# An encoder block's recurrent half: two-tensor work taken from GpSimd to VectorE, its steps dealt anew over eight chunks

## The chip, the core and the metric

The kernel runs on one core of a Trainium2 chip. TensorE (PE) multiplies matrices; VectorE (DVE), ScalarE (ACT) and GpSimd (POOL) work elementwise; SyncE (SP) issues most of the transfers. Each of them executes its own list of instructions in order and waits on semaphores. The metric is the device time of one execution in microseconds. Three runs of the kernel before gave 1787.31, 1787.67 and 1789.67 us: the median is 1787.67 us.

## What is computed

One encoder block on 512 tokens of width 2048. An RMS-normalised input is projected by one wide matrix into the inputs of two branches: a bidirectional recurrent branch (RWKV-7, 16 heads of 64 channels) and a grouped-query attention branch. Both are gated, projected and merged, and a last projection, a residual and a norm follow. The change lies in the recurrent branch. Cut to what matters:

```python
def _wkv_step(S, inp):                       # S: 64 x 64 state of a head and a direction
    w, kk, b, k, v, r = inp
    sa = jnp.einsum('dbhvk,dbhk->dbhv', S, -kk)
    S = S * w[..., None, :] + sa[..., None] * b[..., None, :] + v[..., :, None] * k[..., None, :]
    o = jnp.einsum('dbhvk,dbhk->dbhv', S, r)
    return S, o
...
    kkh = kkh * lax.rsqrt(jnp.maximum(jnp.sum(kkh * kkh, axis=-1, keepdims=True), 1e-24))
    k_eff = _heads(k[None] * (1.0 + (a - 1.0) * k_a.astype(f32)))
    seq_in = (decay, kkh, kkh * ah, k_eff, vh, rh)   # each for both directions
    _, outs = lax.scan(_wkv_step, S0, seq_in)
    wkv = outs[0] + jnp.flip(outs[1], axis=1)
    mu = jnp.mean(wkv, axis=-1, keepdims=True)
    var = jnp.mean(jnp.square(wkv - mu), axis=-1, keepdims=True)
    gn = (wkv - mu) * lax.rsqrt(var + GN_EPS)
...
    return x + jnp.einsum('btd,de->bte', merged, w_out)
```

## The kernel before

**The dense stream.** The wide projection is a stream of products of 128x128 by 128x512 (line 291, tile `acc`). Each weight tile `raw` of four 128x128 blocks is split into a high part `wh` (ACT, line 264) and a rest `wl` (DVE, line 265); twelve products use one such tile, and three tiles of each kind are kept. A *planner* (class `Weave`) writes the PE's order out by hand: each task of the recurrent branch is a generator that yields a cost in planner nanoseconds, a wait, and a flag it needs, and wherever no task is due the planner puts a dense product. The order of DVE, ACT, POOL and SP is made by a scheduler from the order in which the code issues instructions.

**The recurrent branch** goes over eight tiles of 128 channels (two heads), two directions, and eight chunks of 64 tokens:

- `stage_a(i)` makes the decay sums, keys and rates of tile i. `pss` (line 507) sums squares for the key norm, `prb` (516) spreads it. Its elementwise work is cut into seven steps. For tile 0 they run by themselves; for tile i+1 step n runs within chunk n of tile i. `exclusive` (528), `rate` (541), `keys` (544) and the sum of keys (592) are operations with two tensors on POOL; the three exponentials (549 to 551) are on ACT, the products into `BK` (562) on DVE.
- `tile_task(i)` starts with products into `AL` (618 on DVE; 621 on DVE for one direction, on POOL for the other), then `lr` (633) with masks on DVE (636 to 640), a split of `ks` whose rest `cl_` is made on POOL, and a triangular inversion of 60 small DVE operations in series (676, 677) that ends in `XX` (691, 694), which `pq` (709) reads. Then comes the loop over chunks: `pa` (747) reads the state `SV`; ACT copies its result into `a0s` (749, 750), which `pu` (756) reads; ACT copies that into `SV` (757, 758), which `px` (763) reads; DVE makes the next state from it in four operations (769). POOL puts the values of a chunk into `SV` (742) and clears its state part at the start (736, 737).
- `stage_e(i)` norms the output of tile i while tile i+1 is under way: a chain of DVE, ACT and POOL operations that ends in `ow` (802), which the PE transposes (`pg`, 809).

**What sets places around the change.** `OPT` has planner waits: `gn` is the time between the norm's issue and `pg`, `subwait` that between the inversion's transposes and `pq`. `behind(mv, mn, mo)` tells the scheduler to issue a step after three given instructions: the last write of values, the last state operation and the last output copy.

Of the kernel before, what the change touches and what calls it, by code (L numbers as in the profile page):

```python
# [8 lines left out]
F32 = mybir.dt.float32  # L9
# [10 lines left out]
C = 64  # L20
# [190 lines left out]
        return True  # L211


OPT = dict(manual=True, tls=True, sub="dve", subwait=46000, fwait=6000, gn=15000, u1=0, u2=0, c1=700, c2=700, c3=1400, fly=3, scale='pool', prb=4, low=1300, warm=24, rwt='tile', every=2, auto=1, man=1)


def context(nc):
# [7 lines left out]
def emit_all(nc, tc, A, out, dbg):  # L225
# [263 lines left out]
    def stage_a(i):  # L489
# [11 lines left out]
        sq = temp("sq")  # L501
        ac.activation(sq, k, AF.Square, scale=pc(P_KK + i))
        ac.activation(kk, k, AF.Copy, scale=pc(P_KK + i))
        yield 0, 1500, None
        pss = g_tile("pss")
        for tt in range(4):
            pe.matmul(pss[:, 2 * tt:2 * tt + 2], lhsT=sq[:, tt * 128:(tt + 1) * 128], rhs=hs2, start=True, stop=True)
# [12 lines left out]
        def scan(d):  # L520
            h["cs", d] = temp("cs0") if d == 0 else rw.tile([128, T], F32, name="cs1")
            ve.tensor_tensor_scan(h["cs", d], rst, la[:, d], 0.0, ALU.mult, ALU.add)
            if d == 1:
                cs = h["cs", 1]
                ve.tensor_tensor(out=ch(cs), in0=ch(cs)[:, :, C - 1:C].to_broadcast([128, NC, C]), in1=ch(cs), op=ALU.subtract)

        def exclusive(d):
            po.tensor_tensor(out=la[:, d], in0=h["cs", d], in1=la[:, d], op=ALU.subtract if d == 0 else ALU.add)  # L528

            h["in", d], h["ex", d] = (h["cs", d], la[:, d]) if d == 0 else (la[:, d], h["cs", d])  # L530

        def effective(d):
            if d == 0:
                h["ks"] = rw.tile([128, T], F32, name="ks", bufs=2)
                h["BK"] = rw.tile([128, 2, NC, 128], F32, name="BK", tag="bko")
                h["PC"] = rw.tile([128, 2, NC], F32, name="PC", bufs=2)
            h["ke", d] = h["ks"] if d == 0 else temp("ke1")
            ve.tensor_scalar(out=h["ke", d], in0=la[:, 2 + d], scalar1=pc(P_KA + i), scalar2=oka[:, i:i + 1], op0=ALU.mult, op1=ALU.add)

        def rate(d):  # L540
            po.tensor_tensor(out=la[:, 2 + d], in0=la[:, 2 + d], in1=kk, op=ALU.mult)

        def keys(d):
            po.tensor_tensor(out=h["ke", d], in0=h["ke", d], in1=k, op=ALU.mult)

        def exps(d):
            ci, ce = h["in", d], h["ex", d]
            h["e2", d] = rw.tile([128, T], F32, name=f"e2{d}")
            ac.activation(h["e2", d], ci, AF.Exp, scale=-HS)
            ac.activation(ci, ci, AF.Exp, scale=HS)  # L550
            ac.activation(ce, ce, AF.Exp, scale=-HS)

        def ends(d):
            e2 = ch(h["e2", d])
# [3 lines left out]
        def decayed(d, s0):  # L558
            src = la[:, 2 + d] if s0 == 0 else h["ke", d]
            for h0 in (0, 64):  # L560
                sl = s0 if h0 == 0 else 1 - s0
                ve.tensor_tensor(out=h["BK"][h0:h0 + 64, d, :, sl * C:(sl + 1) * C], in0=ch(src)[h0:h0 + 64], in1=ch(h["in", d])[h0:h0 + 64], op=ALU.mult)

        def step(n):
            if n == 0:
                ve.tensor_scalar(out=la, in0=la, scalar1=0.5, scalar2=0.5, op0=ALU.mult, op1=ALU.add)
                scan(0)
            elif n == 1:
                exclusive(0)
                scan(1)  # L570
                effective(0)
            elif n == 2:
                exps(0)
                exclusive(1)
                keys(0)
                effective(1)
                rate(0)
            elif n == 3:
                exps(1)
                keys(1)  # L580
                rate(1)
                decayed(0, 0)
                ends(0)
            elif n == 4:
                ends(1)
                decayed(0, 1)
            elif n == 5:
                decayed(1, 0)
            else:
                decayed(1, 1)  # L590
                ks = h["ks"]
                po.tensor_tensor(out=ks, in0=ks, in1=h["ke", 1], op=ALU.add)
                ve.scalar_tensor_tensor(out=ks, in0=r, scalar=pc(P_RK + i), in1=ks, op0=ALU.mult, op1=ALU.mult)
                fact[i] = (kk, ks, [(h["ex", d], h["e2", d]) for d in range(2)], h["BK"], h["PC"])
                W.flag(f"A{i}", 4000)
# [11 lines left out]
    def tile_task(i):  # L607
# [7 lines left out]
        for d in range(2):  # L615
            e1, e2 = dirs[d]
            for h0, eo, sl in ((0, 0, 0), (64, 1, 1)):
                ve.scalar_tensor_tensor(out=AL[h0:h0 + 64, d, :, eo, sl * C:(sl + 1) * C], in0=ch(kk)[h0:h0 + 64], scalar=-1.0,
                                        in1=ch(e1)[h0:h0 + 64], op0=ALU.mult, op1=ALU.mult)
            for h0, eo, sl in ((0, 0, 1), (64, 1, 0)):  # L620
                (po if d else ve).tensor_tensor(out=AL[h0:h0 + 64, d, :, eo, sl * C:(sl + 1) * C], in0=ch(r)[h0:h0 + 64], in1=ch(e2)[h0:h0 + 64], op=ALU.mult)
        yield 0, OPT['fwait'], None

        LB = rw.tile([128, 2, NC, C], F32, name="LB", tag="lb")
# [27 lines left out]
        VT = rw.tile([128, 4, 128], F32, name="VT", bufs=1)  # L652
        ac.copy(VT, pv.rearrange("p (j c) -> p j c", j=4))
        ch_, cl_ = temp("ch_", F32R), temp("cl_", F32R)
        split(ch_, cl_, ks, po)

        FT = rw.tile([128, 2, NC, 32], F32, name="FT", tag="ft")
        for q in range(4):
# [68 lines left out]
        yield 450, 0, f"N{i + 1}" if i < NT - 1 else None  # L727

        O = rw.tile([128, 2, 2 * NC, C], F32, name="O", tag="lb")
        SV = None  # L730
        for n in range(NC):
            cc = (n, NC - 1 - n)
            both = slice(n, 2 * NC - n, 2 * NC - 1 - 2 * n)
            if SV is None:
                SV = rw.tile([128, 2, 2, 2, C], F32, name="SV", bufs=2)
                po.memset(SV[0:64, :, 0, 0, :], 0.0)
                po.memset(SV[64:128, :, 1, 0, :], 0.0)
            for d in range(2):
                rv = (cc[d] % 2) * 64
                for eo, v0 in ((0, 64), (1, 0)):  # L740
                    src = VT[rv:rv + 64, cc[d] // 2, eo * C:(eo + 1) * C]
                    mv = po.tensor_scalar(out=SV[v0:v0 + 64, d, eo], in0=src.unsqueeze(1).to_broadcast([64, 2, C]),  # L742
                                     scalar1=1.0, scalar2=0.0, op0=ALU.mult, op1=ALU.add)
            pa = c_tile("pa").rearrange("p (d e x) -> p d e x", d=2, e=4)
            for d in range(2):
                for eo in range(2):
# [15 lines left out]
                for eo in range(2):  # L762
                    pe.matmul(px2[:, d, eo, :], lhsT=L2[:, d, cc[d], eo, :], rhs=SV[:, d, eo, 1, :], start=True, stop=True)  # L763
            if n < NC - 1:
                SN = rw.tile([128, 2, 2, 2, C], F32, name="SV", bufs=2)
                for d in range(2):
                    for eo in range(2):
                        h = slice(64 * eo, 64 * eo + 64)
                        mn = ve.scalar_tensor_tensor(out=SN[h, d, eo, 0, :], in0=SV[h, d, eo, 0, :], scalar=PC[h, d, cc[d]:cc[d] + 1], in1=px2[h, d, eo, :], op0=ALU.mult, op1=ALU.add)  # L769
                SV = SN  # L770
# [393 lines left out]
```

## Time and profile before

| | |
|---|---|
| median of three runs | 1787.67 us |
| profiled execution | 1786.3 us |
| its span, first to last instruction | 1784.5 us |
| PE busy | 1708.5 us (96%) |
| DVE busy | 1215.2 us (68%) |
| ACT busy | 849.6 us (48%) |
| POOL busy | 494.7 us (28%) |
| mean granted clock of the PE | 0.982 |

The recurrent stage with its chunk loops lies between about 60 and 1190 us; attention with the rest of the dense stream follows, and the last projection ends the program. A tile of the recurrent stage takes about 132 us. Products overlap in the PE, so that a busy PE can still run at half its clock; the granted clock has to be read beside the busy time.

### The profile page before, as it was taken

To read this page: it belongs to the slowest core of one execution; us is meant where nothing else is said; L and a number is where in the kernel's file an instruction comes from. 1 tells how busy PE (TensorE), PEld (TensorE's weight loads), DVE (VectorE), ACT (ScalarE), POOL (GpSimd) and SP (SyncE) were. 2 spreads that over 40 slices of the span, in tenths; PEclk is the share of its full clock that TensorE was granted. 3 is DMA by queue.
4 is the path that set the end of the run, shared out by engine and by line. 5 is a ranking of instruction groups with operands and counts; after the bars stand their busy time and mean duration, and the time that the engine had idled before them with its cause. 6 is when DMAs were issued, how large, how long until landed. Compare 5 with 4: busy or idle time off the path is not lost.

```text
span 1784.5 us, 26149 instructions
## 1 busy us (share of the span) xinstructions
PE 1708.5 (96%) x8972; PEld 1433.3 (80%) x8972; DVE 1215.2 (68%) x2356; ACT 849.6 (48%) x1955; POOL 494.7 (28%) x604
## 2 busy tenths in 40 slices
PE   7999998999999989999999999999999999999997
PEld 6788877887877877887877877888787888788886
DVE  6567768769779778768668768634878876543342
ACT  5555445355355355455445354444567655332241
POOL 2021051051051061061051051013546542431110
PEclk8999999999999999999999999999999999999999
DMA  6563323313323313324323323325424322434452
GB/s 217 160 204 118 100 63 95 112 55 111 98 64 112 102 54 113 95 54 119 97 57 106 101 60 95 110 71 164 128 77 148 107 91 82 149 113 147 131 181 106
DMA packets 96852, 194.89 MB, mean 109 GB/s; under 512 B 11088, under 2 KB 11344, under 8 KB 95312
## 3 DMA queue, kind: packets, MB, share of 16 engines
q1 hardware_dynamic: 77616, 152.18, 29.4%
q10 hardware_dynamic: 15264, 28.46, 4.5%
q0 software_dynamic: 3840, 12.59, 2.4%
q8 instruction: 72, 1.18, 0.3%
q14 instruction: 60, 0.49, 0.1%
HBM read 162.77 MB, written 30.41 MB: 108 GB/s over the span
## 4 chain that ended last, share of the span: by engine, by line
PE 52%; DVE 6%; ACT 2%; issue 2%; DMA 1%; POOL 1%; POOLq 0%; DVEq 0%; ACTq 0%
PE acc L291 33%; PE of L1095 2%; PE of L1096 2%; PE of L1094 2%; PE px L763 2%; PE po L986 2%; PE pT L971 1%; PE pa L747 1%; DVE wl L265 1%; PE pu L756 1%; PE sc L954 1%; PE sc L955 1%; PE acc L1094 1%; PE acc L1096 1%; PE acc L1095 1%
## 5 line engine op out<-in xcount | busy, mean ns | idle before, releaser
L291 PE MATMUL acc<-hh,wl 128*128 128x512 f32 (+1 forms) x1388 | 555.0, 400 | 2.8 <-DVE wl L265 2.6
L291 PE MATMUL acc<-hl,wh 128*128 128x512 f32 (+1 forms) x1388 | 554.4, 399 | 2.4 <-DVE hl L386 2.1
L291 PE MATMUL acc<-hh,wh 128*128 128x512 f32 (+1 forms) x1388 | 555.7, 400 | 0.0
L265 DVE TENSOR_TENSOR wl<-raw,wh 128x512 fp32r<-128x512 f32 x441 | 340.3, 774 | 282.0 <-ACT wh L264 261.9
L264 ACT CAST wh<-raw 128x512 fp32r<-128x512 f32 x472 | 291.8, 620 | 458.1 <-PE acc L291 314.8
L291 PEld LDWEIGHTS acc<-hh,wl 128*128 128x128 f32 x1388 | 265.5, 191 | 54.7 <-DVE wl L265 5.2
L291 PEld LDWEIGHTS acc<-hl,wh 128*128 128x128 f32 x1388 | 265.4, 191 | 53.5 <-DVE hl L386 3.5
L291 PEld LDWEIGHTS acc<-hh,wh 128*128 128x128 f32 x1388 | 265.5, 191 | 49.9 <-ACT wh L264 0.3
L742 POOL TENSOR_SCALAR SV<-VT 64x128 f32<-64x128 f32 x256 | 123.8, 484 | 584.7 <-DVE SV L769 261.4
L769 DVE SCALAR_TENSOR_TENSOR SV<-SV,PC,px 64x64 f32<-64x64 f32 x224 | 62.7, 280 | 68.2 <-PE px L763 51.1
L676 DVE TENSOR_TENSOR tm<-B 128x30 f32<-128x30 f32 (+14 forms) x240 | 82.1, 342 | 4.8
L291 PE MATMUL acc<-oq,wh 128*128 128x512 f32 x256 | 83.1, 396 | 2.0 <-ACT oq L1018 1.3
L677 DVE TENSOR_TENSOR B<-B,tm 128x30 f32<-128x30 f32 (+14 forms) x240 | 79.0, 329 | 5.4
L747 PEld LDWEIGHTS pa<-SV,AL 128*128 128x128 f32 x512 | 67.7, 191 | 16.5 <-POOL la L528 8.5
L747 PE MATMUL pa<-SV,AL 128*128 128x64 f32 x512 | 67.4, 271 | 9.4 <-DVE SV L769 9.4
L1095 PE MATMUL of<-wl,mh 128*128 128x512 f32 x192 | 74.9, 390 | 0.2
L1096 PE MATMUL of<-wh,ml 128*128 128x512 f32 x192 | 74.7, 389 | 0.0
L763 PEld LDWEIGHTS px<-SV,L 128*128 128x128 f32 x512 | 68.6, 195 | 7.1 <-ACT SV L757 1.6
L1094 PE MATMUL of<-wh,mh 128*128 128x512 f32 x192 | 66.1, 389 | 0.0
L763 PE MATMUL px<-SV,L 128*128 128x64 f32 x512 | 66.0, 273 | 0.1
L771 ACT COPY O<-px 64x128 f32<-64x128 f32 x64 | 16.7, 261 | 100.4 <-DVE SV L769 89.9
L756 PEld LDWEIGHTS pu<-a0s,XP 128*128 128x128 f32 x256 | 37.1, 194 | 25.1 <-ACT a0s L750 20.4
(687 smaller groups left out, 2844.9 us busy)
## 6 DMA issues: line engine op xcount, KB each, us to landing
raw<-in_w_in_dram SPq DMA_DIRECT2D x344, 256.0 KB, 3.2
raw<-in_wo_dram SPq DMA_DIRECT2D x64, 256.0 KB, 2.8
fsp<-tg ACTq DMA_DIRECT2D x60, 256.0 KB, 2.4
tsp<-la ACTq DMA_DIRECT2D x32, 256.0 KB, 3.6
la<-tsp SPq DMA_DIRECT2D x8, 1024.0 KB, 5.6
raw<-in_wbr_dram SPq DMA_DIRECT2D x32, 256.0 KB, 3.1
tgm<-fsp POOLq DMA_DIRECT2D x32, 256.0 KB, 3.6
raw<-in_wba_dram SPq DMA_DIRECT2D x32, 256.0 KB, 2.9
```

Of the source, the lines that this page charges most:

```text
L264: ac.copy(dst_hi, src)
L265: (eng or ve).tensor_tensor(out=dst_lo, in0=src, in1=f(dst_hi), op=ALU.subtract)
L291: pe.matmul(acc[:, tok], lhsT=w[1 if u == 2 else 0][:, j, :], rhs=(xl if u == 1 else xh)[:, kt, tok], start=(kt == 0 and u == 0 and tok.st ...
L676: se.tensor_tensor(out=tv, in0=B[:, 0:s, s:s + 1].to_broadcast([128, s, n]), in1=B[:, s:s + 1, s + 1:32].to_broadcast([128, s, n]), op=ALU ...
L677: se.tensor_tensor(out=B[:, 0:s, s + 1:32], in0=B[:, 0:s, s + 1:32], in1=tv, op=ALU.add)
L742: mv = po.tensor_scalar(out=SV[v0:v0 + 64, d, eo], in0=src.unsqueeze(1).to_broadcast([64, 2, C]), scalar1=1.0, scalar2=0.0, op0=ALU.mult, ...
L747: pe.matmul(pa[:, d, eo, :], lhsT=AL[:, d, cc[d], eo, :], rhs=SV[:, d, eo, 0, :], start=True, stop=True)
L763: pe.matmul(px2[:, d, eo, :], lhsT=L2[:, d, cc[d], eo, :], rhs=SV[:, d, eo, 1, :], start=True, stop=True)
L769: mn = ve.scalar_tensor_tensor(out=SN[h, d, eo, 0, :], in0=SV[h, d, eo, 0, :], scalar=PC[h, d, cc[d]:cc[d] + 1], in1=px2[h, d, eo, :], op0 ...
L1094: pe.matmul(acc, lhsT=mh[:, dt, tok(tt)], rhs=w[0], start=(dt == 0), stop=False)
L1095: pe.matmul(acc, lhsT=mh[:, dt, tok(tt)], rhs=w[1], start=False, stop=False)
L1096: pe.matmul(acc, lhsT=ml[:, dt, tok(tt)], rhs=w[0], start=False, stop=(dt == NKT - 1))
```

## The change

All operations with two tensors that POOL did in `stage_a` and `tile_task` are issued on DVE: `exclusive`, `rate`, `keys`, the sum of keys, the second direction of the `AL` products and the rest `cl_` of the split. For each tile these are ten operations (two, two, two, one, two, one); POOL keeps the values of the state, the 8-column copies `PC`, small powers and its transfers. The seven steps are dealt anew: two exponentials of a direction stay together in `exp_in`, the third of both directions goes to step 4 (`exp_ex`); `exclusive(1)` stays in step 2, `rate` moves one step later. The values of chunk n+1 are written (`state`) ahead of the state operations of chunk n, and the steps are issued behind these writes. Three planner waits grow: `gn` from 15000 to 22000, `subwait` from 46000 to 47000, and for tile 0 the wait ahead of `pss` from 1500 to 6000.

```diff
-OPT = dict(..., subwait=46000, fwait=6000, gn=15000, ...)
+OPT = dict(..., subwait=47000, fwait=6000, gn=22000, ...)
...
-        yield 0, 1500, None
+        yield 0, 1500 if i else 6000, None
...
         def exclusive(d):
-            po.tensor_tensor(out=la[:, d], in0=h["cs", d], in1=la[:, d], op=ALU.subtract if d == 0 else ALU.add)
+            ve.tensor_tensor(out=la[:, d], in0=h["cs", d], in1=la[:, d], op=ALU.subtract if d == 0 else ALU.add)
...
-            po.tensor_tensor(out=la[:, 2 + d], in0=la[:, 2 + d], in1=kk, op=ALU.mult)
+            ve.tensor_tensor(out=la[:, 2 + d], in0=la[:, 2 + d], in1=kk, op=ALU.mult)
...
-            po.tensor_tensor(out=h["ke", d], in0=h["ke", d], in1=k, op=ALU.mult)
+            ve.tensor_tensor(out=h["ke", d], in0=h["ke", d], in1=k, op=ALU.mult)
...
-        def exps(d):
-            ci, ce = h["in", d], h["ex", d]
+        def exp_in(d):
+            ci = h["in", d]
             h["e2", d] = rw.tile([128, T], F32, name=f"e2{d}")
             ac.activation(h["e2", d], ci, AF.Exp, scale=-HS)
             ac.activation(ci, ci, AF.Exp, scale=HS)
-            ac.activation(ce, ce, AF.Exp, scale=-HS)
+
+        def exp_ex(d):
+            ac.activation(h["ex", d], h["ex", d], AF.Exp, scale=-HS)
...
+            elif n == 2:
+                exp_in(0)
+                exclusive(1)
                 effective(0)
-            elif n == 2:
-                exps(0)
-                exclusive(1)
                 keys(0)
                 effective(1)
+            elif n == 3:
+                exp_in(1)
+                ends(0)
                 rate(0)
-            elif n == 3:
-                exps(1)
                 keys(1)
+                decayed(0, 0)
+            elif n == 4:
+                exp_ex(0)
+                exp_ex(1)
+                ends(1)
                 rate(1)
-                decayed(0, 0)
-                ends(0)
-            elif n == 4:
-                ends(1)
                 decayed(0, 1)
...
-                po.tensor_tensor(out=ks, in0=ks, in1=h["ke", 1], op=ALU.add)
+                ve.tensor_tensor(out=ks, in0=ks, in1=h["ke", 1], op=ALU.add)
...
-                (po if d else ve).tensor_tensor(out=AL[h0:h0 + 64, d, ...], in0=ch(r)[h0:h0 + 64], in1=ch(e2)[h0:h0 + 64], op=ALU.mult)
+                ve.tensor_tensor(out=AL[h0:h0 + 64, d, ...], in0=ch(r)[h0:h0 + 64], in1=ch(e2)[h0:h0 + 64], op=ALU.mult)
...
-        split(ch_, cl_, ks, po)
+        split(ch_, cl_, ks)
...
+        def state(n):
+            new = rw.tile([128, 2, 2, 2, C], F32, name="SV", bufs=2)
+            for d, c in ((0, n), (1, NC - 1 - n)):
+                ...
+                    mv = po.tensor_scalar(out=new[v0:v0 + 64, d, eo], in0=src.unsqueeze(1).to_broadcast([64, 2, C]),
+                                          scalar1=1.0, scalar2=0.0, op0=ALU.mult, op1=ALU.add)
+            return new, mv
+
+        SV, _ = state(0)
...
-                SN = rw.tile([128, 2, 2, 2, C], F32, name="SV", bufs=2)
+                SN, mv = state(n + 1)
```

**How it moves the work.** DVE, chunk loop of the third tile (the one whose trace stands below around 501 us), from the third state update on. `SV` is the next state, `la` holds sums and rates, `cs` the running sums, `ks` and `ke` the keys, `BK` products for the next tile. Before:

```order
L769 SCALAR_TENSOR_TENSOR SV<-SV,PC,px_4656 64x64 x4
L538 TENSOR_SCALAR ke_4674<-la,par,der 128x512
L265 TENSOR_TENSOR wl<-raw,wh 128x512
L769 SCALAR_TENSOR_TENSOR SV<-SV,PC,px_4717 64x64 x4
L562 TENSOR_TENSOR BK<-la,cs_4547 64x8x64 x2
L265 TENSOR_TENSOR wl<-raw,wh 128x512 x2
L769 SCALAR_TENSOR_TENSOR SV<-SV,PC,px_4782 64x64 x4
L562 TENSOR_TENSOR BK<-ks,cs_4547 64x8x64 x2
L265 TENSOR_TENSOR wl<-raw,wh 128x512
```

The changed kernel at the same place:

```order
L776 SCALAR_TENSOR_TENSOR SV<-SV,PC,px_4679 64x64 x4
L528 TENSOR_TENSOR la<-cs_4637,la 128x512
L538 TENSOR_SCALAR ks<-la,par,der 128x512
L538 TENSOR_SCALAR ke_4704<-la,par,der 128x512
L544 TENSOR_TENSOR ks<-ks,k 128x512
L265 TENSOR_TENSOR wl<-raw,wh 128x512
L776 SCALAR_TENSOR_TENSOR SV<-SV,PC,px_4749 64x64 x4
L541 TENSOR_TENSOR la<-la,kk 128x512
L544 TENSOR_TENSOR ke_4704<-ke_4704,k 128x512
L564 TENSOR_TENSOR BK<-la,cs_4582 64x8x64 x2
L265 TENSOR_TENSOR wl<-raw,wh 128x512
```

Between the third and the fourth state update stand five instructions where two stood; `exclusive` (528), `keys` (544) and `rate` (541) are those that came from POOL.

ACT in the same loop, after the fourth chunk's output copies; `e` takes an exponential, `a0s` is what `pu` waits for. Before:

```order
L771 COPY O<-px_4717 64x2x64
L772 COPY O<-px_4717 64x2x64
L549 ACTIVATE e_4729<-la 128x512
L551 ACTIVATE cs_4609<-cs_4609 128x512
L476 DMA fsp<-tg 128x512
L749 COPY a0s<-pa 64x128
L750 COPY a0s<-pa 64x128
```

The changed kernel:

```order
L778 COPY O<-px_4749 64x2x64
L779 COPY O<-px_4749 64x2x64
L549 ACTIVATE e_4765<-la 128x512
L550 ACTIVATE la<-la 128x512
L756 COPY a0s<-pa 64x128
L757 COPY a0s<-pa 64x128
```

The exponential of `cs` is gone from this place (it stands a chunk later now, beside that of the other direction), and the one that stood among the copies stands ahead of them.

DVE in the inversion of the fourth tile, around the norm's last operation, `ow` (802 before, 809 now; `tm` and `B` are the inversion's). Before:

```order
L305 SCALAR_TENSOR_TENSOR k<-acc,par,k 128x511
L676 TENSOR_TENSOR tm<-B 128x84
L306 SCALAR_TENSOR_TENSOR k<-acc,par,k 128x511
L677 TENSOR_TENSOR B<-B,tm 128x3x28
L802 TENSOR_TENSOR ow<-ow,s_5135 128x512
L265 TENSOR_TENSOR wl<-raw,wh 128x512
```

The changed kernel:

```order
L265 TENSOR_TENSOR wl<-raw,wh 128x512
L680 TENSOR_TENSOR tm<-B 128x84
L681 TENSOR_TENSOR B<-B,tm 128x3x28
L680 TENSOR_TENSOR tm<-B 128x108
L681 TENSOR_TENSOR B<-B,tm 128x4x27
L809 TENSOR_TENSOR ow<-ow,s_5165 128x512
L680 TENSOR_TENSOR tm<-B 128x130
L265 TENSOR_TENSOR wl<-raw,wh 128x512
```

`ow` stands one pair of the inversion and one weight tile later in DVE's order. In the PE's order `pg` stood 33 dense products behind the last transpose of `BK` in tiles 1 to 7, and stands 64 behind it now; `pq` stands five dense products later in each tile, `pss` of tile 0 twenty.

## Rows read from the trace of the kernel before

**Rows 1.** The page, part 1: busy us (share of the span) x instructions.
```profile
PE 1708.5 (96%) x8972; PEld 1433.3 (80%) x8972; DVE 1215.2 (68%) x2356; ACT 849.6 (48%) x1955; POOL 494.7 (28%) x604
```
**Rows 2.** Waits of PE, whole span: who <- releaser: total us, times, longest us.
```profile
PE pg L809 <- DVE ow L802: 22.9, 7, 3.9
PE pu L756 <- ACT a0s L750: 12.5, 14, 1.6
PE pa L747 <- DVE SV L769: 9.4, 5, 2.5
...
PE pss L507 <- ACT sq L502: 3.8, 1, 3.8
```
**Rows 3.** Windows behind two waits: length, busy (count) PE PEld DVE ACT POOL, granted clock, DMA.
```profile
307.60:317.60 10.00, 9.93 (x41) 8.21 (x42) 8.24 (x20) 4.51 (x9) 0.76 (x1) 0.83 0.34 99
703.50:713.50 10.00, 8.92 (x31) 7.22 (x32) 7.75 (x18) 3.80 (x8) 0.84 (x2) 0.66 0.35 102
```
**Rows 4.** Timeline, norm of tile 2: start, us, engine, line, [idle before <- releaser].
```profile
565.71 1.33 POOL L265 TENSOR_TENSOR cl__5179<-ks,ch__5178 128x512 fp32r<-128x512 f32 x1 [6.30 <-issue]
565.81 1.25 DVE L800 TENSOR_SCALAR s<-s 128x8 f32<-128x8 f32 x1
...
566.96 0.39 PE L291 MATMUL acc<-hh,wl 128*128 128x512 f32 x1
...
567.19 0.39 PE L291 MATMUL acc<-hh,wh 128*128 128x512 f32 x1
...
569.59 0.68 DVE L802 TENSOR_TENSOR ow<-ow,s 128x512 f32<-128x512 f32 x1
...
570.41 1.50 PE L809 MATMUL pg<-con,ow 128*64 128x128 f32 x7 [2.83 <-DVE ow L802]
```
**Rows 5.** Timeline, chunk loop of the third tile, third state update.
```profile
501.03 4.43 DVE L265 TENSOR_TENSOR wl<-raw,wh 128x512 fp32r<-128x512 f32 x1 [0.40 <-ACT wh L264]
501.13 1.27 POOL L544 TENSOR_TENSOR ks<-ks,k 128x512 f32<-128x512 f32 x1
...
503.61 1.30 POOL L528 TENSOR_TENSOR la<-cs,la 128x512 f32<-128x512 f32 x1
...
505.49 1.22 DVE L769 SCALAR_TENSOR_TENSOR SV<-SV,PC,px 64x64 f32<-64x64 f32 x4
...
505.91 1.35 PE L747 MATMUL pa<-SV,AL 128*128 128x64 f32 x8 [1.56 <-DVE SV L769]
```
**Rows 6.** Timeline, chunk loop of the fourth tile, exponentials and `pu`.
```profile
647.23 0.63 ACT L549 ACTIVATE e<-la 128x512 f32<-128x512 f32 x1
647.43 0.69 DVE L562 TENSOR_TENSOR BK<-la,cs 64x512 f32<-64x512 f32 x1
...
647.66 1.36 POOL L742 TENSOR_SCALAR SV<-VT 64x128 f32<-64x128 f32 x3
...
648.79 0.63 ACT L550 ACTIVATE la<-la 128x512 f32<-128x512 f32 x1
...
649.89 0.55 PE L756 MATMUL pu<-a0s,XP 128*128 128x64 f32 x3 [1.01 <-ACT a0s L750]
```
**Rows 7.** Groups by line and form, POOL, 100 to 1180 us: busy, mean ns.
```profile
L742 POOL TENSOR_SCALAR SV<-VT 64x128 f32<-64x128 f32 x248 | 120.7, 487 | 576.0 <-DVE SV L769 253.2 <-ACT VT L653 142.6 <-PE acc L291 113.8
```
**Rows 8.** Windows: from `lr`'s masks to `XX`, and six chunks of the third tile.
```profile
545.20:611.30 66.10, 63.27 (x315) 52.21 (x314) 59.94 (x135) 29.99 (x64) 8.22 (x12) 0.97 0.35 101
...
491.50:530.20 38.70, 35.12 (x211) 30.18 (x210) 26.54 (x44) 19.10 (x62) 22.83 (x33) 1.00 0.22 64
```
**Rows 9.** Timeline of PE and of DVE: `lr` of the fourth tile, its `XX` and `pq`.
```profile
542.22 2.06 PE L633 MATMUL lr<-AL,BK 64*128 64x128 f32 x32
...
610.70 0.59 DVE L691 COPY XX<-RR 32x256 f32<-32x256 f32 x2
...
612.20 0.98 PE L709 MATMUL pq<-XX,LQ 128*128 128x32 f32 x8
```
**Rows 10.** Timeline of ACT in `stage_a` of tile 0, ahead of `pss`.
```profile
84.56 0.63 ACT L549 ACTIVATE e<-la 128x512 f32<-128x512 f32 x1 [4.43 <-POOL la L528]
```

More of the change, by code (lines that the diff above doesn't have):

```diff
@@ L211, in step @@
         return True
-OPT = dict(manual=True, tls=True, sub="dve", subwait=46000, fwait=6000, gn=15000, u1=0, u2=0, c1=700, c2=700, c3=1400, fly=3, scale='pool', prb=4, low=1300, warm=24, rwt='tile', every=2, auto=1, man=1)
+OPT = dict(manual=True, tls=True, sub="dve", subwait=47000, fwait=6000, gn=22000, u1=0, u2=0, c1=700, c2=700, c3=1400, fly=3, scale='pool', prb=4, low=1300, warm=24, rwt='tile', every=2, auto=1, man=1)
 def context(nc):
@@ L620, in tile_task @@
             for h0, eo, sl in ((0, 0, 1), (64, 1, 0)):
-                (po if d else ve).tensor_tensor(out=AL[h0:h0 + 64, d, :, eo, sl * C:(sl + 1) * C], in0=ch(r)[h0:h0 + 64], in1=ch(e2)[h0:h0 + 64], op=ALU.mult)
+                ve.tensor_tensor(out=AL[h0:h0 + 64, d, :, eo, sl * C:(sl + 1) * C], in0=ch(r)[h0:h0 + 64], in1=ch(e2)[h0:h0 + 64], op=ALU.mult)
         yield 0, OPT['fwait'], None
@@ L729, in tile_task @@
         O = rw.tile([128, 2, 2 * NC, C], F32, name="O", tag="lb")
-        SV = None
+        def state(n):
+            new = rw.tile([128, 2, 2, 2, C], F32, name="SV", bufs=2)
+            for d, c in ((0, n), (1, NC - 1 - n)):
+                rv = (c % 2) * 64
+                for eo, v0 in ((0, 64), (1, 0)):
+                    src = VT[rv:rv + 64, c // 2, eo * C:(eo + 1) * C]
+                    mv = po.tensor_scalar(out=new[v0:v0 + 64, d, eo], in0=src.unsqueeze(1).to_broadcast([64, 2, C]),
+                                          scalar1=1.0, scalar2=0.0, op0=ALU.mult, op1=ALU.add)
+            return new, mv
+        SV, _ = state(0)
+        po.memset(SV[0:64, :, 0, 0, :], 0.0)
+        po.memset(SV[64:128, :, 1, 0, :], 0.0)
         for n in range(NC):
@@ L733, in tile_task @@
             both = slice(n, 2 * NC - n, 2 * NC - 1 - 2 * n)
[L734 to L743, printed above, removed]
             pa = c_tile("pa").rearrange("p (d e x) -> p d e x", d=2, e=4)
```

## The prediction, made before the changed kernel was timed

> **What bounds the kernel now.** I read the busy lines first: PE is busy 96% of the span, DVE 68%, ACT 48%, POOL 28% [rows 1]. The change adds no product and takes none away, so what it can gain is bounded by the time in which PE waits or runs slowly. The list of PE's waits comes next [rows 2]. Four of its groups have a releaser that the change touches: `pg` waits seven times, 22.9 us in all, for the norm's `ow` on DVE; `pu` fourteen times, 12.5 us, for `a0s` on ACT; `pa` five times, 9.4 us, for the state on DVE; `pss` once, 3.8 us, in tile 0. That is 48.6 us.
>
> A wait costs more than its length. PE's clock has two levels, 1.2 and 2.4 GHz, and behind a long wait the trace shows stretches at the lower one. The 10 us behind `pg` of the second tile were granted 0.83 of the full clock, those behind `pg` of the fifth 0.66 [rows 3]: a sixth and a third of the products' time there, so 1.7 and 3.4 us lost on top of waits of 3 to 4 us. Read so, five of the seven `pg` waits have the smaller loss and two the larger (5 × 1.7 + 2 × 3.4 = 15.3 us), two of the five `pa` waits the larger (6.8 us), and the wait of `pss` the smaller (1.7 us). The `pu` waits, all under 1.7 us, have none. So 48.6 + 23.8 = 72.4 us are at stake, 4% of the time.
>
> **The change part by part: pg.** Row by row [rows 4]: PE has run its dense products, two of them 0.23 us apart, and comes to `pg` 2.83 us before it may start; `ow` is the last of a chain on DVE, ACT and POOL, and one of that chain's operations, on eight columns, took 1.25 us, ending together with POOL's `cl_`, which had started 0.10 us before it. The changed order puts `pg` 64 dense products behind the last transpose where it had 33: 31 × 0.23 = 7.1 us later on PE. `ow` moves back too, but less: one weight tile and now `cl_` stand ahead of it on DVE, at 0.7 us each (`ow` itself, of the same shape, took 0.68), while up to 1.1 of the 1.25 us return when POOL's `cl_` is gone. So `ow` comes 0.3 to 1.4 us later, `pg` 7.1 us later, and the longest wait, 3.9 us, turns into a margin of at least 7.1 − 1.4 − 3.9 = 1.8 us. All of 22.9 + 15.3 = 38.2 us goes. What is late next: the weight tile `wl` that follows `ow` on DVE is wanted by products that stand about ten places (2.3 us) ahead of `pg`, so they may wait for it in place of `pg`, 0 to 1.2 us. I take 0.4 for each of seven tiles, nearer to nothing because that is also nearer to what the margin allows: 2.8 us given back.
>
> **pa.** All five waits stand at the same chunk of a tile, where three operations of two tensors follow each other on POOL. In the third tile [rows 5] `wl` on DVE starts 0.10 us ahead of POOL's `ks` and takes 4.43 us, ending with the third POOL operation; with it the state update is late by almost 4 us, and PE waits 1.56 us. The change takes these operations from POOL, where each took 1.27 to 1.30 us, to DVE, where the products into `BK` with as many elements took 0.69 [rows 6]. What held `wl` is then gone, and so are these waits: 9.4 + 6.8 = 16.2 us. The price is DVE's: ten operations a tile, 6.9 us, of which six stand in the chunk loop (4.1 us) against 3.7 us that the one held `wl` gives back there. That cover holds as long as DVE has idle time in the loop. Six chunks of the third tile lasted 38.7 us with DVE idle 12.2 us of it [rows 8], 6.4 us a chunk. The fullest chunk of the new order has five operations of 0.69, two of 0.75 at most and the 1.22 us of the state, 6.2 us; without the wait a chunk is about 5.8 us. So DVE would be some 0.4 us late in one or two chunks, and in [rows 5] a state almost 4 us late made PE wait only 1.56. I take no wait; the worst is 0.4 us twice in seven tiles, 5.6 us. If that cover were gone, all 6.9 us a tile would show, which is the last rival below.
>
> **pu.** ACT has exponentials and weight casts between the output copies and `a0s` [rows 6]: with four such items, two of which stand in the rows at 0.63, `pu` waited 1.01 us. With one item of 0.63 fewer it would wait 0.4, with two fewer nothing. In the changed order I find, over the seven tiles, six places with three items and one with four: 6 × 0.4 + 1.0 = 3.4 us stay, and 12.5 − 3.4 = 9.1 go. POOL's writes of values, 487 ns in the mean of 248 [rows 7], now stand ahead of the state operations, and POOL has nothing between them that is as long as the 1.3 us operations, so they cost nothing; they were never PE's releaser.
>
> **pss and pq.** In tile 0 twenty dense products (20 × 0.23 = 4.6 us) now run ahead of `pss`, more than its 3.8 us: 3.8 + 1.7 = 5.5 go. `pq` follows the inversion on DVE, the stretch where DVE is fullest: 59.94 us of 66.10 in the fourth tile [rows 8]. There `lr` stands at 542.22, `XX` ends at 611.29 and `pq` starts at 612.20 [rows 9]: 0.91 us to spare, the least of the eight tiles. PE loses 2.83 and 1.7 us of its way from `lr` to `pq` and gets five products more: 69.98 − 2.83 − 1.7 + 1.15 = 66.6 us. DVE loses 1.1 and gets 0.7 for `cl_`: 69.07 − 0.4 = 68.7 us if it keeps all 6.16 us of its idle time, and 62.5 without it. So `pq` waits between 2.1 us and nothing. DVE's idle in this stretch is to a good part waiting for `wh`, whose buffers PE frees; when PE is faster, that time shrinks with it. I take 0 for the forecast and keep the 2.1 for a rival.
>
> In `stage_a` of tile 0 an exponential waited 4.43 us for POOL's `la` [rows 10]; on DVE that is 0.69 instead of 1.3, which only helps `pss`.
>
> **The sum.** 38.2 (`pg`) + 16.2 (`pa`) + 9.1 (`pu`) + 5.5 (`pss`) = 69.0; less 2.8 it is 66.2 us. The profiled execution lasted 1786.3 us, so 1720.1; it lies 1.4 us below the median of the three runs, so I forecast **1721.5 us**. Its own range is 1714 (every wait of the four groups gone) to 1735 (the price of `wl` at 1.2 × 7, the 5.6 us of late states, and one small clock loss in two tiles).
>
> **The rivals.** First, *DVE becomes the bound between `lr` and `pq`*. The same stretch is at 91% on DVE, PE gets shorter there, DVE hardly. Then `pq`, or the `wl` ahead of `pg`, waits some 2.1 us, and a wait of that size may take the clock down for 1.7 to 3.4 us more, as waits of 3 to 4 us did [rows 3]. For the tightest tile alone that is 3.8 us, for seven tiles 27 to 39 us; the others have more to spare, so I put the case at 10 to 39 us and its middle at 1746. For it speaks the 91%, against it that DVE's idle is partly PE's doing. Chance 0.22.
>
> Second, *the change doesn't do what it says in the chunk loop*: the waits of `pa` and `pu` come back in other chunks, since DVE's list there is now longer and ACT's no shorter. Only `pg` and `pss` gain: 1721.5 + 16.2 + 9.1 = 1747 us. The held `wl` speaks against it. Chance 0.09.
>
> Third, *the moved operations are held on DVE by POOL's writes of values*, which read `VT` while they write. In [rows 6] a `BK` product of 0.69 ran from 647.43 to 648.12 with three such writes beginning at 647.66, and was no longer than it is elsewhere; the writes were, three in 1.36 us against 0.487 each. If it were DVE that was held, with 0.3 us for each of four writes of a chunk, the two fullest chunks of a tile would be 1.2 us late: 7 × 2 × 1.2 = 17 us, 1738. Chance 0.04. The Trainium skill, "SBUF — State Buffer", section "Who interferes with whom", gives such a rule: a VectorE instruction with two SBUF inputs contends with a GpSimd instruction that reads SBUF, and the one that issues first keeps the shared ports. The held `wl` of [rows 5] agrees with the contention, though it started first and ended last.
>
> Fourth, the one on the other side: *every moved operation lengthens DVE's chain of a tile*. If DVE, not PE, sets a tile's length once POOL's help is gone, then the 2.1 us of `pq`, the 1.1 us that don't come back, and nine operations at 0.69 are 2.1 + 1.1 + 6.2 = 9.4 us a tile, with a clock loss of 3.4 behind them 12.8; seven tiles make 90 us against a gain of 66, so 1811 us. It decides from 66.2 / 7 = 9.5 us of DVE's time a tile. DVE's 91% in the stretch speaks for it, the 12.2 us of idle in six chunks against it. Chance 0.05. The Trainium skill, "Perfetto Trace Analysis", section "Optimizing Scalar/DVE Operations", speaks for this one: it suggests taking work off a saturated DVE, to GpSimd even, and adds that the shared port may make that useless; here it is the second half that [rows 5] bear out.
>
> **How the numbers follow.** Forecast 0.60, rivals 0.22, 0.09, 0.04 and 0.05. The time is the forecast's. The range runs from 1714 to 1753: it holds the forecast's range, the second and third rivals and most of the first, and leaves out the last, the top of the first, and a little on either side. About 0.2% (3.6 us) is what a measurement of this kernel can tell from no change. Faster takes all cases but the last, less 0.03 for one that loses what it gains: 0.92; same 0.03; slower 0.05.
>
> **What would show it.** In the profile after, PE's list of waits should have no `pg`, no `pa`, no `pss` and some 3 us of `pu`, and a few waits of products for `wl` near `pg`; no 10 us of the stage should be granted less than 0.9. On DVE no `wl` of the loop should last over 1 us, and POOL should have no operation on two tensors there. Waits of `pq` show the first rival, `pa` or `pu` at other chunks the second, `BK` or `ks` products over 1 us beside the writes of values the third, DVE busy through whole tiles the fourth. The forecast is wrong if PE's waits shrink by the sum but the clock stays low in places: then the losses behind waits were priced as going with them and do not.

## The result, and the profile after

The changed kernel took 1745.22 us (median of three runs, 1742.30 to 1746.14) against 1787.67: a ratio of 0.9756, with a 95% interval of 0.9734 to 0.9778. The forecast was 1721.5 us; its own range, 1714 to 1735, ended 10 us below the result, and the wider one, 1714 to 1753, held it. Two thirds of the forecast gain came: 42.5 of 66.2 us. The profiled execution is the one of 1745.22 us.

The page, busy us (share of the span) x instructions, answers to [rows 1]:

```profile
PE 1694.3 (97%) x8972; PEld 1423.0 (82%) x8972; DVE 1212.0 (70%) x2437; ACT 849.1 (49%) x1955; POOL 393.4 (23%) x523
```

The span is 1743.5 us, 41.0 less. PE's idle time, the span without its busy time, went from 76.0 to 49.2 us (26.8 less), and its busy time from 1708.5 to 1694.3 (14.2 less) although it does the same products: that second part is clock, whose mean grant rose from 0.982 to 0.990. POOL is busy 101 us less, and DVE, to which the work went, 3 us less.

The waits of PE over the whole span (who <- releaser: total us, times, longest us) answer to [rows 2]:

```profile
PE pss L507 <- ACT sq L502: 6.9, 3, 3.1
PE pu L763 <- ACT a0s L757: 6.2, 14, 1.1
...
PE acc L291 <- DVE wl L265: 4.0, 2, 3.5
PE acc L291 <- ACT oah L264: 3.4, 1, 3.4
...
PE acc L291 <- DVE tgm L1067: 2.1, 1, 2.1
```

`pg` and `pa` are gone from the list, 32.3 us of waits. `pu` is halved. Two things are new: `pss` waits three times, in later tiles than tile 0, and products of the attention part wait 3.4 us for `oah` (the rounded output of the attention heads) and 2.1 us for `tgm` (a gate read back from memory; 0.4 before). The wait of 3.5 us for `wl` stands there too, where the longest was 1.5 before. Windows of 10 us behind the longest of them (length, busy and count of PE, PEld, DVE, ACT and POOL, granted clock, DMA) answer to [rows 3]:

```profile
689.00:699.00 10.00, 10.00 (x41) 8.10 (x41) 8.86 (x23) 1.82 (x4) 1.74 (x1) 0.83 0.34 94
945.00:955.00 10.00, 10.00 (x43) 8.24 (x44) 8.67 (x23) 1.24 (x2) 2.01 (x2) 0.83 0.28 81
1239.00:1249.00 10.00, 10.00 (x42) 8.15 (x42) 7.46 (x15) 6.95 (x15) 6.68 (x6) 0.83 0.46 132
1471.00:1481.00 10.00, 5.92 (x13) 4.20 (x14) 4.37 (x6) 2.90 (x5) 5.44 (x6) 0.53 0.40 131
```

Of the ten slow stretches between 60 and 1190 us two are left, both behind a `pss` wait; two stand in the attention part, where there were none.

What `pss` waits for is seen in the timeline of the fifth tile (start, us, engine, line, idle before <- releaser):

```profile
675.41 0.74 DVE L306 SCALAR_TENSOR_TENSOR k<-acc,par,k 128x511 f32<-128x511 f32 x1
...
684.89 0.74 DVE L819 SCALAR_TENSOR_TENSOR gc<-gc,par,ks 128x512 f32<-128x512 f32 x1
...
686.52 0.74 DVE L820 SCALAR_TENSOR_TENSOR gc<-gc,par,sz 128x512 f32<-128x512 f32 x1
...
687.30 0.72 ACT L502 ACTIVATE sq<-k,par 128x512 f32<-128x512 f32 x1 [2.53 <-DVE gc L820]
...
688.08 1.05 PE L507 MATMUL pss<-con,sq 128*128 128x2 f32 x8 [2.83 <-ACT sq L502]
```

`sq` is the square of `k`, and `k` is ready at 676.15. But `sq` starts only when the norm of the tile before has finished with `gc` and `sz`, at 687.26. These are temporaries: `sq`, `gc`, `sz` and others share four buffers, and the reading is that `sq` gets one that the norm must give back; e3 below tests it. The norm's end follows `pg`, and `pg` was moved back by 31 products. In this tile `pss` stands only 16 products behind `pg`, in the two others that wait 22 and 14; where it stands 43 to 47 behind, three times, it doesn't wait.

The end of the attention part, on all engines:

```profile
1468.82 0.74 PE L993 MATMUL po<-pl,VS 128*128 128x256 f32 x4
1469.60 0.58 ACT L997 COPY ov<-po 64x512 f32<-64x512 f32 x1 [1.56 <-PE po L993]
1470.22 0.69 DVE L998 TENSOR_TENSOR oa<-po,ov 64x512 f32<-64x512 f32 x1 [1.45 <-ACT ov L997]
1471.04 1.26 POOL L1001 TENSOR_TENSOR oa<-oa,re 128x512 f32<-128x512 f32 x1 [5.80 <-DVE oa L998]
1472.33 0.62 ACT L264 CAST oah<-oa 128x512 fp32r<-128x512 f32 x1 [2.15 <-POOL oa L1001]
...
1473.00 1.22 PE L291 MATMUL acc<-oah,wh 128*128 128x512 f32 x2 [3.44 <-ACT oah L264]
```

Behind the last `po` (a product of the attention heads) the next product in PE's order needs the last `oah`, and PE waits through a chain of four operations on three engines.

### The profile page after: what moved, and what is told of

The parts are those of the page before. It is cut to its first block, busy times and chain, and to the rows that moved or that the text cites. A ratio compares the mean times of both kernels' runs of the same rounds, so it can differ in the third digit from the quotient of the medians.

```text
span 1743.5 us, 26135 instructions
## 1 busy us (share of the span) xinstructions
PE 1694.3 (97%) x8972; PEld 1423.0 (82%) x8972; DVE 1212.0 (70%) x2437; ACT 849.1 (49%) x1955; POOL 393.4 (23%) x523
## 5 line engine op out<-in xcount | busy, mean ns | idle before, releaser
L265 DVE TENSOR_TENSOR wl<-raw,wh 128x512 fp32r<-128x512 f32 x442 | 316.4, 718 | 240.2 <-ACT wh L264 216.6
L741 POOL TENSOR_SCALAR SV<-VT 64x128 f32<-64x128 f32 x256 | 137.4, 537 | 622.7 <-DVE SV L776 262.6
L754 PEld LDWEIGHTS pa<-SV,AL 128*128 128x128 f32 x512 | 66.7, 191 | 4.8
L770 PE MATMUL px<-SV,L 128*128 128x64 f32 x512 | 64.7, 269 | 0.0
L291 PE MATMUL acc<-oah,wh 128*128 128x512 f32 x128 | 52.1, 409 | 5.5 <-ACT oah L264 3.4
```

What stands on the lines that cost most here:

```text
L291: pe.matmul(acc[:, tok], lhsT=w[1 if u == 2 else 0][:, j, :], rhs=(xl if u == 1 else xh)[:, kt, tok], start=(kt == 0 and u == 0 and tok.st ...
L741: mv = po.tensor_scalar(out=new[v0:v0 + 64, d, eo], in0=src.unsqueeze(1).to_broadcast([64, 2, C]), scalar1=1.0, scalar2=0.0, op0=ALU.mult, ...
L754: pe.matmul(pa[:, d, eo, :], lhsT=AL[:, d, cc[d], eo, :], rhs=SV[:, d, eo, 0, :], start=True, stop=True)
```

## The experiments

Every kernel below but e2 is an edit of the changed one, and most from e5 on are edits of e4. The result of each is the median of four runs, e1 to e4 on one chip and the others on a second; the kernel before, run beside them, gave 1788.9 to 1789.9 us, 1 to 2 us above the first three runs, so differences of 3 us and more between them are read, smaller ones not.

**The two halves apart.** The three planner waits set PE's order and nothing else does: with the old waits the changed code has PE's order of before, and with the new waits the old code has that of after. So each half can be run alone. The changed code with the old waits, e1:

```diff
-OPT = dict(..., subwait=47000, ..., gn=22000, ...)
+OPT = dict(..., subwait=46000, ..., gn=15000, ...)
-        yield 0, 1500 if i else 6000, None
+        yield 0, 1500, None
```

> The changed kernel with the three planner waits as they were (gn 15000, subwait 46000, pss of tile 0 1500): PE's order is that of the kernel before, only DVE, ACT and POOL have the new one. Theory that the two halves add up: pg waits as before (7 waits, 23 to 28 us, with half-clock stretches behind them), no pa waits, pu waits about 6 us, no pss waits in later tiles, the attention part as before (waits about 4 us): 1787.7 - 16.2 (pa with its clock) - 6.3 (pu) = 1765 us. Rival, that the moved work makes ow later: pg waits grow by 1 us each and more take the larger clock loss: 1775 to 1780 us.

It took 1756.8 us, 0.9826 of the kernel before (0.9806 to 0.9847), 8 us better than the sum of the terms. Its waits of PE:

```profile
PE pg L816 <- DVE ow L809: 21.1, 7, 3.8
PE pu L763 <- ACT a0s L757: 6.8, 15, 0.9
...
PE pss L507 <- ACT sq L502: 1.5, 1, 1.5
```

The moved work took all `pa` waits, half of `pu`, and also 2.3 us of `pss` in tile 0 and 1.8 of `pg`, so `ow` did not come later. The last 3 us are clock: behind only one `pg` wait a window of 10 us was granted 0.66, behind five 0.83, behind the last 1.00.

The code of before with the new waits alone, the reverse edit on the other kernel, e2:

> The kernel before with the three new planner waits alone: PE's order is that of the changed kernel, the operations stay on POOL. Theory that the halves add up: no pg waits (38.2 us gone) and no pss wait in tile 0 (5.5 gone), but pss waits in three later tiles (6.9 + 3.4 us) and some 13 us more in the attention part, pa and pu waits as before: 1787.7 - 43.7 + 10.3 + 13 = 1767 us. Rival, that the new PE order pays only with POOL unloaded: pg still waits because POOL's cl_ holds the norm, over 1775 us.

It took 1772.9 us, 0.9915 (0.9894 to 0.9936). Its waits:

```profile
PE pu L756 <- ACT a0s L750: 11.8, 14, 1.6
PE pss L507 <- ACT sq L502: 9.5, 3, 4.1
...
PE pa L747 <- DVE SV L769: 5.6, 3, 1.9
...
PE acc L291 <- ACT oah L264: 3.4, 1, 3.4
```

`pg` no longer waits here either, so its waits were a matter of PE's order and not of POOL's `cl_`. The new `pss` and `oah` waits are here too, `pss` longer than in the changed kernel. So they come with the planner waits; the moved work doesn't cause them, it only shortens `pss`. Two of the five `pa` waits are gone as well with the planner waits alone, so the halves overlap: they gain 32 and 16 us apart, 42 to 44 together.

**A buffer of its own for sq (e3).**

```diff
-        sq = temp("sq")
+        sq = rw.tile([128, T], F32, name="sq", bufs=1)
```

> The changed kernel with one edit: sq has a buffer of its own, not one of the four that temporaries share. PE's order is the same. Theory that sq waits for the buffer that the norm's gc (read last by DVE at L820) gives back: the three pss waits (6.9 us) and the half-clock stretches behind two of them (3.4 us) go, 1745.2 - 10.3 = 1735 us. Rival, that k itself is late on the full DVE: pss waits stay, 1745 us.

It took 1735.0 us, 0.970 (0.968 to 0.972): 10.3 us less than the changed kernel, as the waits and their clock made it. Between the profiled spans it is 9.3 us: 6.9 of idle time, and 2.4 of busy time instead of the 3.4 of two slow stretches, because the stretch behind the attention part's first wait was granted 0.66 here where it had 0.83. No `pss` wait is left. The waits of the attention part are as they were; PE's between 1160 and 1550 us:

```profile
PE acc L291 <- DVE wl L265: 3.6, 1, 3.6
PE acc L291 <- ACT oah L264: 3.4, 1, 3.4
PE acc L291 <- DVE tgm L1067: 2.0, 1, 2.0
PE pT L978 <- DVE st__12579 L968: 1.2, 1, 1.2
...
```

**The dense products given back to the attention part (e4).** Each longer wait in the recurrent stage is filled with dense products, which then no longer stand in the attention part. Ahead of the first attention product stood 3782 of line 291's 4932 products before, and 3854 after. Here two waits go back on top of the edit of e3: `subwait` in all tiles, and `gn` in the last tile, whose `pg` had 11.6 us to spare.

```diff
-OPT = dict(..., subwait=47000, ...)
+OPT = dict(..., subwait=46000, ...)
-        yield 0, OPT['gn'], None
+        yield 0, OPT['gn'] if i < NT - 1 else 15000, None
```

> As e3, and the dense products that the longer waits took from the attention part are given back: subwait 46000 as before, and gn 15000 for the norm of the last tile alone, so that 3784 dense products stand ahead of the attention (3854 in the changed kernel, 3782 before). Theory that the attention part lacks products to cover its chains: its waits (17 us with the weights') shrink to about the 4 us of before and the half-clock stretches at 1239 and 1471 us go, 1735 - 13 = 1722 us. Rival, that these waits come of how the attention's own steps happen to fall: about 1735 us, perhaps with waits at other places. pq has 1.4 us to spare in the tightest tile and loses 1.1, so no pq wait by either.

It took 1721.7 us, 0.9622 (0.960 to 0.9645): 13.3 us less again, and the best version but for e6, which can't be told from it. The page's busy line, and PE's waits:

```profile
PE 1684.3 (98%) x8972; PEld 1414.6 (82%) x8972; DVE 1207.7 (70%) x2436; ACT 848.1 (49%) x1955; POOL 398.4 (23%) x524
```

```profile
PE pu L763 <- ACT a0s L757: 5.2, 12, 0.9
...
PE prb L516 <- DVE rb L512: 2.1, 3, 1.5
PE acc L291 <- ACT oq L1025: 1.4, 1, 1.4
```

The waits for `oah` and `tgm` are gone, and no slow stretch is left between 25 and 1700 us. Its span is 1719.7 us: against the kernel before, PE's idle time is 40.6 us less and its busy time 24.2 us less. The prediction had 42.4 us of waits and 23.8 us of clock. So with these two repaired the sum comes out as predicted, in waits and in clock; what the changed kernel lacks are two things that the prediction had not looked at.

**Stock or step?** Two more points on the number of dense products ahead of the attention, both with `sq`'s own buffer and `gn` as in the changed kernel: `subwait` 46000 (e9, 3817 products) and 48000 (e10, 3889).

> The kernel of e3 (sq with its own buffer) with subwait 46000: 3817 dense products stand ahead of the attention, between e4 (3784, 1721.7 us) and e3 (3854, 1735.0 us). Theory that the dense products are a stock, each one used earlier missing later at about 0.2 us: 1735.0 - 37 x 0.19 = 1728 us. Rival, that e3's waits in the attention part come of one unlucky order: 1722 or 1735 us, or anything not between.

> The kernel of e3 with subwait 48000: 3889 dense products ahead of the attention, 35 more than in e3. Theory of the stock: the attention part gets 35 x 0.23 = 8 us more waits, 1742 us. Rival: no more waits there than in e3, 1735 us.

They took 1735.5 us (0.970) and 1735.2 us (0.9695), both the same as e3. So a dense product used earlier has no price of its own: 72 products more or less between these three change nothing, while e9 and e4, which differ in the last norm's wait alone, lie 13.9 us apart. Where the waits stand changes. Those of e9:

```profile
PE acc L291 <- ACT oq L1025: 4.3, 1, 4.3
PE acc L291 <- ACT oah L264: 3.0, 1, 3.0
...
PE acc L291 <- DVE tgm L1067: 2.1, 1, 2.1
```

What goes with the time is how many dense products (line 291) the order leaves behind the last `po`: 375 before and in e1, 382 in e4, 372 in e12 (below), 342 to 344 in the changed kernel, e2, e3, e9 and e10. Those five all show a wait of 3.0 to 3.4 us for `oah` and one of some 2 us for `tgm`; the other four have none for `oah` and at most 0.4 us for `tgm`. So it looks like a step: with some thirty more products behind the last `po` the end of the attention part is covered. Why the planner lands on one side or the other is not shown by these runs, and a value of the last `gn` in between was not tried.

**The moved work, its engine and its dealing.** Three kernels take one thing back from e4 each, with PE's order unchanged: the engine (e5, all ten operations on POOL), the early values (e6), and the dealing of the steps over the chunks (e7).

```diff
-            ve.tensor_tensor(out=la[:, d], in0=h["cs", d], in1=la[:, d], ...)
+            po.tensor_tensor(out=la[:, d], in0=h["cs", d], in1=la[:, d], ...)
...
-        split(ch_, cl_, ks)
+        split(ch_, cl_, ks, po)
```

> The kernel of e4 (1721.7 us) with the ten operations of a tile back on POOL; PE's order, the new dealing and the early values stay. Theory that the move itself pays in the loop: wl on DVE is held again beside POOL's operations, now at most two in a chunk (up to 2.6 us instead of 4), so pa or pu waits come back, 5 to 16 us in all: 1727 to 1738 us; no pg waits, because ow has 3.4 us to spare. Rival, that the new dealing took the waits away and the engine matters little: 1722 us.

1730.1 us (0.9664, 0.9637 to 0.9692), 8.4 us more than e4, with no `pa` wait:

```profile
PE pu L763 <- ACT a0s L757: 7.0, 12, 0.9
...
PE prb L516 <- DVE rb L512: 4.3, 4, 2.0
```

3.6 us more of idle time and 4.6 us more of busy time make it up. The busy part isn't clock, for both kernels were granted 0.996; what it is was not followed up. `wl` is still held in the loop, up to 1.95 us where e4 has at most 0.92. But in the new dealing there are at most two POOL operations in a chunk, and that is not enough to make `pa` wait. The edit for the values:

```diff
-                SN, mv = state(n + 1)
+                SN = rw.tile([128, 2, 2, 2, C], F32, name="SV", bufs=2)
...
+            mv = state(n, SV)
             pa = c_tile("pa").rearrange(...)
```

> The kernel of e4 with the writes of a chunk's values back behind the state operations. Theory of the prediction, that these writes are never what PE waits for: 1722 us, no new wait. Rival, that values behind the state operations and behind the steps come late for px: waits of pa or px in most of the 64 chunks, 0.3 us each, 1735 to 1740 us.

1720.7 us (0.9612, 0.9589 to 0.9636): the same as e4. The order of the values is worth nothing here. For the dealing, the branches of the step list and the three exponentials were put back as the change's diff has them on its minus side.

> The kernel of e4 with the steps dealt over the chunks as before (three exponentials of a direction together, rate a step earlier); operations stay on DVE. Theory that pu waits for exponentials between ACT's copies and pa for held DVE operations: pu waits back to about 12 us from 5.2, no pa waits, 1729 us. Rival, that the old dealing also overfills DVE in a chunk (seven operations in one step): pa waits come back in each tile, over 1735 us.

1725.0 us (0.9635, 0.9612 to 0.9658), 3.3 us more than e4, and no `pa` wait. `pu` is the only wait that grew, by 5.3 us; others shrank a little, so that PE's idle time is 2.2 us more and its busy time 1.4. The longest `pu` wait, 1.44 us, had a window granted 0.83 behind it, where the prediction took the `pu` waits to cost no clock:

```profile
PE pu L759 <- ACT a0s L753: 10.5, 14, 1.4
```

Then engine and dealing were both put back (e11):

> The kernel of e4 with both the ten operations back on POOL and the old dealing; early values, sq's buffer and PE's order stay. Theory that the pa waits need both, three POOL operations in a row and their place beside a wl: pa waits back, 5 to 9 us with up to 7 us of clock, pu about 10 us: 1721.7 + 8.4 (e5) + 3.3 (e7) + 8 to 14 = 1741 to 1747 us. Rival, that e5 and e7 simply add: 1733 us.

1740.9 us (0.9732, 0.9713 to 0.975), 19.2 us more than e4, where the two alone add 11.7. `pa` waits again, twice, and behind each wait is a slow stretch. Ahead of the first a `wl` on DVE took 3.58 us (355.78 to 359.36) beside three POOL operations in a row, as in [rows 5]:

```profile
PE pu L759 <- ACT a0s L753: 9.2, 12, 1.4
PE prb L516 <- DVE rb L512: 4.4, 4, 2.0
...
PE pa L750 <- DVE SV L772: 3.7, 2, 1.9
```

```profile
359.00:369.00 10.00, 9.18 (x32) 7.84 (x32) 4.40 (x11) 3.97 (x12) 4.55 (x7) 0.54 0.18 52
...
746.00:756.00 10.00, 7.91 (x29) 6.55 (x30) 4.51 (x8) 3.97 (x12) 5.34 (x8) 0.66 0.19 49
```

So a `pa` wait needs both: the operations on POOL, and the old dealing that sets three of them in a row. Either of the two, the engine or the dealing, alone takes the waits away.

e11 also divides e4's gain. It keeps PE's order and `sq`'s buffer, and of the rest only the early values, which e6 found to be worth nothing: 48 of the 67 us are those of PE's order with that buffer, and 19 those of the move and the new dealing together.

**DVE's cover (e8).** Seven of the ten moved operations of a tile are issued a second time, into a tile that nobody reads:

```diff
             ve.tensor_tensor(out=la[:, 2 + d], in0=la[:, 2 + d], in1=kk, op=ALU.mult)
+            ve.tensor_tensor(out=sq, in0=la[:, 2 + d], in1=kk, op=ALU.mult)
```

> The kernel of e4 with seven of the moved operations (those of the chunk loop and of the sum of keys) issued twice on DVE, the second one into a scratch tile that nobody reads: 7 x 0.69 = 4.8 us more DVE work a tile. Theory that PE sets the tile's length and DVE's idle time covers most: only the fullest chunks are late, some 1 us in two chunks of seven tiles, 1722 to 1736 us. Rival (the prediction's fourth), that DVE's work sets the tile's length: 4.8 us in each of seven tiles and clock losses behind, 1755 us or more.

1722.2 us (0.9619, 0.9595 to 0.9643), the same as e4, with 35 us more work on DVE:

```profile
PE 1685.0 (98%) x8972; PEld 1415.1 (82%) x8972; DVE 1242.6 (72%) x2492; ACT 849.5 (49%) x1955; POOL 399.1 (23%) x524
```

**What is left of pu and prb (e12).**

```diff
-OPT = dict(..., c1=700, ...)
+OPT = dict(..., c1=900, ...)
-        yield 250, 4500, None
+        yield 250, 5200, None
```

> The kernel of e4 with the planner's wait ahead of pu at 900 instead of 700 and that ahead of prb at 5200 instead of 4500. By the theory that PE's waits are all that is left: pu's 5.2 us shrink to 1 or 2, prb's 2.1 us go, nine products fewer for the attention cost some 2 us: 1717 to 1720 us. Rival, that ACT's and DVE's lists move with it and give the waits back: 1722 us.

1723.2 us (0.9629, 0.9615 to 0.9643), no gain on e4: `pu` waits 5.9 us and `prb` 1.5. A longer planner wait ahead of `pu` did not shorten `pu`'s waits; why was not followed up.

## Why the prediction was right, and where it was too high

Against the forecast gain of 66.2 us the changed kernel has 42.5. The wide range held the result, but partly by luck: its upper end was there for the first two rivals, and neither came; what took 24 us from the gain was in no rival. The narrow range, the forecast's own, missed it. (By the terms named for it, that range adds up to 1715 to 1736, not 1714 to 1735; nothing hangs on the 1 us.) Two of the signs failed with it: PE's list has `pss`, and two windows of the recurrent stage were granted 0.83. The working of the sum, term by term:

- **pg, 38.2 us: right.** No `pg` wait and no slow stretch behind one; `ow` now ends 3.9 us or more ahead of `pg` in every tile, where the prediction had a margin of at least 1.8. e2 shows that PE's order alone does it. The 2.8 us set aside for `wl` near `pg` were too many: one such wait of 0.5 us stands in the recurrent stage.
- **pa, 16.2 us: right** in size and in place. No `wl` on DVE is held any more, where one took 4.43 us [rows 5]; between 100 and 1180 us (count: min/median/max ns, first and last start):

```profile
L265 DVE TENSOR_TENSOR wl<-raw,wh x293: 641/691/781, 102.0 to 1179.4; 128x512 fp32r<-128x512 f32 x147
```

  In [rows 5] the held `wl` ends 0.55 us behind the third POOL operation (505.46 against 504.91), not with it; the reading that it was held stands. What the prediction did not say is that the dealing alone would have taken these waits away (e5).
- **pu, 9.1 us: mis-sized,** 6.3 came. The prediction counted seven places with three or four items ahead of `a0s` and priced four at 1.0 and three at 0.4; fourteen places wait, 0.4 us in the mean. The longest, 1.08 us, on ACT behind the output copies:

```profile
876.40 0.63 ACT L549 ACTIVATE e<-la 128x512 f32<-128x512 f32 x1
876.93 0.61 ACT L264 CAST wh<-raw 128x512 fp32r<-128x512 f32 x1
877.44 0.68 ACT L304 ACTIVATE v<-acc,der 128x512 f32<-128x512 f32 x1
878.02 0.62 ACT L550 ACTIVATE la<-la 128x512 f32<-128x512 f32 x1
878.54 0.25 ACT L756 COPY a0s<-pa 64x128 f32<-64x128 f32 x1
...
879.11 0.66 PE L763 MATMUL pu<-a0s,XP 128*128 128x64 f32 x4 [1.08 <-ACT a0s L757]
```

  Four items gave 1.08 us, as priced. It is the count of the shorter waits that was too low.
- **pss of tile 0, 5.5 us: right.** But the step "what is late next", which followed `pg` only to `wl`, failed. It looked at what stands ahead of `pg` on PE and not at what waits for the norm's end behind it. Moved back by 31 products, the norm held a buffer that `sq` of the next tile needs, and `pss` took over part of `pg`'s waits: 6.9 us and two slow stretches of 1.7. e3 measures 10.3 us.
- **The attention part, nothing in the sum: 13.3 us** between e3 and e4. The prediction moved dense products ahead of `pg`, `pq` and `pss` at no price, since PE executes each of them once in any order. It did not ask what they had covered. In the last tile the products that fill the longer wait came out of the attention part, where they had stood behind the last `po`.
- **pq, taken at 0: right,** and its way as worked out. In the fourth tile `lr` begins at 521.55, and then:

```profile
585.69 0.59 DVE L695 COPY XX<-RR 32x256 f32<-32x256 f32 x2
...
588.25 0.98 PE L713 MATMUL pq<-XX,LQ 128*128 128x32 f32 x8
```

  PE's way from `lr` to `pq` is 66.7 us (66.6 predicted), DVE's to the end of `XX` 64.7, inside the 62.5 to 68.7 that were left open. DVE's idle time did give way when PE got faster: on the way from `lr` to the end of `XX` it is 4.8 us in 64.7, where it was 6.2 in 69.1.

Together: 66.2 − 10.3 (`pss`) − 13.3 (attention) − 2.8 (`pu`) + 2.3 (`wl`) = 42.1 us, against 42.5 measured between the medians and 41.0 between the spans.

Of the rivals, the first (DVE the bound at `pq`) has no wait to show in the changed kernel. e8 doesn't bear on it, for its additional operations stand outside the stretch from `lr` to `XX`. And e4 is at that bound: in its fifth tile the copy into `XX` that `pq` reads ends at 708.56 and `pq` starts at 708.70, just as close as `pg` stood behind `ow` in its seven waits before. The product ahead of `pq` starts at 708.18, so `pq` is some 0.3 us late (an estimate from the 0.23 us between products): a faster PE would pay there. That the change does not do what it says in the loop is ruled out by the missing `pa`. The third (DVE held by POOL's writes): the moved operations took 0.69 us in the mean, only `keys` 0.77, and it was the writes that became longer, as this row of the changed kernel between 100 and 1180 us shows beside [rows 7]; the second number behind the bar is the mean in ns. With the operations back on POOL (e5) it is 494.

```profile
L741 POOL TENSOR_SCALAR SV<-VT 64x128 f32<-64x128 f32 x256 | 137.4, 537 | 622.7 <-DVE SV L776 262.6 <-ACT VT L657 188.7 <-PE acc L291 138.5
```

The fourth, on the other side, is refuted by e8 for the chunk loop: seven operations more a tile would have been 34 us, and the measured difference is 0.6. The Trainium skill, "Perfetto Trace Analysis", section "Optimizing Scalar/DVE Operations", says that offloading from DVE may make sense if DVE is saturated. At 70% over the span and with e8 free, this one isn't saturated there.

## What to carry to other kernels

When a wait is taken away by issuing its consumer later, look behind it as well as ahead: whatever the late step held, above all a buffer from a shared pool, is given back later too, and the next to ask for it waits. And ask of the work that is pulled forward to fill the gap what it covered where it stood; here one setting for the last tile uncovered the end of another stage and cost 14 us, a third of the gain. A list of an engine's work by chunk is worth drawing up before moving any of it to another engine: here dealing it better took the same `pa` waits away as moving it, though the move was worth another 8.4 us (e5).

## What the runs showed of the hardware

The clock's share was larger than the waits suggest: between the kernel before and e4 24.2 us of 64.8 are busy time of the same products, at a mean granted clock of 0.982 and 0.996. Two `pa` waits of 1.87 us each in e11 were followed by windows granted 0.54 and 0.66, so 4.6 and 3.4 us behind 1.9 us of waiting, while a `pg` wait of 2.06 us in e1 was followed by one at 1.00. And a `pu` wait of 1.44 us in e7 was followed by one at 0.83, one of 1.4 us in e11 by one at 1.00. The length of a wait alone didn't tell which.

An operation of two tensors on DVE that by the trace began 0.10 us ahead of POOL's was held until POOL had done three of its own [rows 5], and yet POOL's writes of values became longer beside DVE's operations (537 ns against 487). The Trainium skill, "SBUF — State Buffer", section "Who interferes with whom", says that the order of issue decides who blocks. The held `wl`, which started first and ended last, doesn't agree with that; the writes of values don't decide it.
